# A two-block transformer on one core: split-ahead loads with three blocks of lead, their stores on ScalarE's queue, and another order in the hybrid block

## The chip, the cores and the metric

The kernel runs on one core of one Trainium2 chip, in one launch. The metric is the time of the program on the device in microseconds (us). It was timed three times: 1630.78, 1632.08 and 1635.72 us, with a median of 1632.08. One more execution was taken with the hardware profiler on; the trace and its page are of that one.

## The reference

The input is one sequence of 256 tokens with 1024 features, all float32. Two ordinary layers come first, then one hybrid layer:

```python
for layer in range(2):
    mix = diff_attention(h, ...) if layer == 0 else moba_attention(h, ...)
    h = layer_norm(alpha * h + mix, ln1_g[layer], ln1_b[layer])
    h = layer_norm(alpha * h + relu(h @ w_up[layer]) ** 2 @ w_down[layer],
                   ln2_g[layer], ln2_b[layer])
# hybrid layer
proj = rmsnorm(x, norm1_gain) @ w_in               # 1024 -> 1720 columns
...                                                # NSA and MLA attention on slices of proj
h = x + concat(rmsnorm(o_a), rmsnorm(o_b)) @ w_out
return h + peer_ffn(rmsnorm(h), w_q, sub_keys, u, v)    # top-16 of 16384 experts
```

Here `w_up` is 1024 x 4096 and `w_down` 4096 x 1024 in each layer. The first 416 columns of `w_in` (in the kernel's own order) are the inputs of MLA's low-rank projections `w_uq` and `w_ukv`, then come 24 gates, 512 columns of compressed keys and values, and 768 of NSA queries and keys.

## The kernel before, in words

**Weights.** Every weight block is 128 rows of up to 1024 float32 columns, 512 KB. To keep float32 accuracy on TensorE (PE), a block is split in two: `whi` is a cast on ScalarE (ACT, L415), `wlo = raw - whi` a subtraction on VectorE (DVE, L417), and each product is three matmuls (hi x hi, lo x hi, hi x lo). All blocks stand in one list, `self.plan`. `load_raw` (L449) keeps four raw blocks loaded or on their way, on SyncE's queue (SP). `pump` (L402) splits the next block whenever one of six `whi`/`wlo` buffer pairs is free. Each engine and each queue runs its instructions in the order in which they are written. A `tick` (L324) stands after each block of PE work; it moves background generators one step on.

**The MLP** (`mlp`, L809) runs once in each of the two layers. The up stage is four groups of eight blocks (`proj_F`, L475 to L495 hold the matmuls of the helpers). After each group ACT and DVE evacuate four banks one after the other (relu, square, split into hi and lo). The down stage has 32 blocks (`proj_T`).

**Split ahead.** While the MLP runs, `split_ahead` (L427) prepares blocks that the hybrid block will need in a hurry: nine in each layer, 18 in all. It loads a raw block on SP (L436), waits two ticks, casts it on ACT (L439) and subtracts on DVE (L441), waits a tick, and stores both parts to DRAM on SP (L445), then waits two ticks. That is five ticks a block; nine blocks take the 45 ticks that the MLP gives it. There is one raw buffer and one `hi` buffer. The raw buffer also takes the low part, so the next load has to wait for the store of it.

**The hybrid block** (`hybrid`, L1234) is a planner. Its work is written as generators whose steps name an engine, a modelled cost, the events that they wait for and PSUM banks. `Flow.run` picks the step that can start first by the model, ties by a rank, and emits it; so the ranks and costs set the order of instructions on each engine, and nothing else does. Ahead of the flow stands LayerNorm of the first half of the tokens and a part of the second half's (`norm_add(1, 0)`). In it, `second_norm` does the rest of the second half, `x_split` makes hi and lo of the normalized, transposed input, `dense` runs the projections (first 440 columns, half of the next 512, `w_uq`, `w_ukv`, the other half, the last 768, called A, B and C in `accA` to `accC`), and `weights` emits loads and splits of the blocks, where those prepared ahead come back from DRAM as `whi` and `wlo` (L1218). `residual` makes the scaled input on GpSimd (POOL) and from it `r1`, the RMS factor that `lora` waits for, whose result `w_uq` and `w_ukv` multiply. Where the model sees a gap on PE, `fill` emits dummy matmuls into a spare bank (L1289).

Of the kernel before, what the change touches and what calls it, by code (L numbers as in the profile page):

```python
# [9 lines left out]
F32 = mybir.dt.float32  # L10
# [10 lines left out]
P = 128  # L21
# [256 lines left out]
class Net:  # L278
# [147 lines left out]

    def split_ahead(self, pool, blocks):  # L427

        nc = self.nc
        for b in blocks:  # L430
            src, _ = self.plan[b]
            n = width(src)
            raw = pool.tile([P, 1024], F32, tag="ahead_l", name="ahead")
            hi = pool.tile([P, 1024], F32R, tag="ahead_h", name="ahead")
            to = raw[:, :n]
            nc.sync.dma_start(out=to if len(src.shape) == 2 else to.rearrange("p (c n) -> p c n", c=2), in_=src)  # L436
            yield
            yield
            nc.scalar.copy(out=hi[:, :n], in_=raw[:, :n])  # L439
            lo = raw.bitcast(F32R)  # L440
            nc.vector.tensor_tensor(out=lo[:, :n], in0=raw[:, :n], in1=hi[:, :n], op=ALU.subtract)  # L441
            yield
            self.pre[b] = [self.dram.tile([P, n], F32, name=f"pre{i}_{b}") for i in range(2)]
            for to, of in zip(self.pre[b], (hi.bitcast(F32), raw)):
                nc.sync.dma_start(out=to, in_=of[:, :n])  # L445
            yield
            yield
# [361 lines left out]
    def mlp(self, layer):  # L809
        nc = self.nc  # L810
        self.mark(f"up{layer}")
        with self.tc.tile_pool(name="mlp", bufs=1) as mp:
            hid = Split(mp, "hid", 32, 8)
            b = self.first_hybrid
            self.ahead = self.split_ahead(mp, [b + 2 + layer, *range(b + 11 + 8 * layer, b + 19 + 8 * layer)])
            calls = []

            def pause():
                calls.append(None)
                self.ahead_on = len(calls) < 4  # L820
# [366 lines left out]
    def weights(self, f, end, more, ready, done, extra, cw_ev):  # L1187
# [8 lines left out]
        for b in range(self.split, end + more):  # L1196
# [10 lines left out]
            if parts:  # L1207
                ev = yield "SP", 0.1, (place,), 0
                t = max(t, ev.t) + n * 0.0032
            else:  # L1210
                t = max(t, split[b - 4].t + 2.0 if b - 4 in split else 0.0) + n * 0.0016
                yield on_act(n, (Ev(t if b >= early else 0.0), place))
            self.free[pool] -= 1
# [20 lines left out]
    def hybrid(self, down):  # L1234
# [12 lines left out]
        with ExitStack() as ctx:  # L1247
# [31 lines left out]
            for sl in (slice(0, 256), slice(256, 1024)):  # L1279
                norm_scale(0, sl)  # L1280
            norm_add(1, 0)

            f = Flow(1)
            spare = self.bank()

# [49 lines left out]
            def second_norm():  # L1335
                ev = yield on_dve(512, (Z,))
                sl = slice(512, 1024)
                stt(out=xn[1][:, sl], in0=old[1][:, sl], scalar=ALPHA, in1=down[1][1], op0=mult, op1=add)
                down[0] = down[1] = None
                f.give(2, ev)  # L1340
                yield on_dve(512)
                nc.vector.bn_stats(out=stats[1][0][:, 1, :], in_=xn[1][:, sl])
                yield "DVE", 1.6, None, 0
                norm_rsqrt(1)
                ev = yield on_dve(256, fast=True)
                norm_scale(1, slice(0, 256))
# [39 lines left out]
            def residual():  # L1386
                evs = []
                for th in range(2):
                    after = () if th == 0 else (scaled[1],)
                    for c in range(0, D, 256):  # L1390
# [67 lines left out]
            def dense():  # L1458
# [25 lines left out]

                yield from second(range(4))
                for th in range(2):
                    for i in range(2):
                        ev = yield on_pe(1.04, (ready[b], ready[b + 1], lo_ev[0], lo_ev[1]), 1)
                        acc = self.bank()
                        for k in range(2):  # L1490
# [3 lines left out]
                                     k == 0, k == 1)  # L1494
                        f.add(uq_evac(th, i, acc, ev), 24.5)
                        del acc, w
# [3 lines left out]
                for th in range(2):  # L1500
# [3 lines left out]
                    for i in range(2):  # L1504
                        sl = slice(i * 512, (i + 1) * 512)
                        self.mm3(acc[i], lo.hi(2)[:, halves[th]], lo.lo(2)[:, halves[th]], w[0][:, sl], w[1][:, sl], True, True)
                    f.add(ukv_evac(th, acc, ev), 0)
                    del acc, w
                release(b, ev)
                b += 1  # L1510
                yield from second(range(4, KD))
                for k in range(KD):
# [17 lines left out]
            def lora():  # L1530
# [19 lines left out]
                gates_ev.t = ev.t  # L1550
                f.add(lora_rms(lss, evs), 31)
                banks = None
# [60 lines left out]
            def mla_norms():  # L1613
# [7 lines left out]
                for h in range(2):  # L1621
                    hl = slice(4 * h, 4 * h + 4)
                    kl = slice(8 + 4 * h, 12 + 4 * h)
                    for th in range(2):
# [3 lines left out]
                        self.scale_heads(kr[th].unsqueeze(1).to_broadcast([P, 4, 32]), r[:, th, kl], mqk[th][:, kl, 64:96])  # L1628
                        f.add(mla_heads(8 + 4 * h, th, ev), 5.5)
                        ev = yield on_dve(384, (ev, rope_ev[1][th]))  # L1630
                        self.scale_heads(mqk[th][:, hl], r[:, th, hl])
                        f.add(mla_heads(4 * h, th, ev), 6)

# [88 lines left out]
            def mla_values():  # L1722
                for c in range(4):
# [7 lines left out]
                    if c % 2 == 1:  # L1731
                        f.add(mla_out(c, ob, ev), 27)
                        del ob
# [24 lines left out]
            def values():  # L1758
# [12 lines left out]
                for kv in range(2):  # L1771
                    f.add(windows(kv, ev, blk_ev[kv]), 3.5)
                f.add(compress(blk_ev), 11.5)

            def windows(kv, ev, out):

                yield on_pe(0.44, (ev,), 1)
                ps = self.bank()
# [324 lines left out]
            f.add(gating(), 9)  # L2103
            for th in range(2):
                f.add(k_rope(th), 41.5)
                f.add(q_rope(th), 16)
            f.add(mla_norms(), 2)
            for i in range(8):
                c = i // 4 * 4
                ops = lambda i=i: (mT[:, i, 0:P], mT[:, i, P:S], mT[:, 8 + i, :])  # L2110
                after = [head_ev[d, th] for d in (c, 8 + c) for th in range(2)] + [exp_ev]
                f.add(head(ops, after, (m_ev, m_used, mts), i), 1.5)
            f.add(mla_values(), 14)
            f.add(values(), 2.5)
            for th in range(2):
                f.add(nsa_evac(th), 16)
            f.add(nsa_norms(), 6.5)
            f.add(compressed(), 0.5)
            for i in range(0, 16, 2):
# [3 lines left out]
                gate = [[gates[th][:, 4 * g + j, 1 + br:2 + br] for th in range(2)] for g in range(2)]  # L2123
                f.add(head_pair(ops, (qk_ev[2], qk_ev[j // 2], gate_ev), (n_ev, n_used, nts), i, gate, nsa_rank), 6.5)
            for j in range(4):
                f.add(nsa_values(j), 3)
            f.add(out_dense("b", range(4, 8), end - 8, b_last), 44.5)
            f.add(out_dense("a", range(4), end - 4, a_last), 6.5)
            f.add(mla_update(), 3)
            f.add(last_rms(), 0)  # L2130
            self.xs = None
# [310 lines left out]
    def make_plan(self):  # L2442
# [67 lines left out]
```

## Time and profile before

| what | before |
|---|---|
| median of 3 runs | 1632.08 us |
| the profiled execution | 1632.38 us |
| its span | 1630.6 us |
| PE busy | 1588.0 us, 97% of the span |
| DVE busy, ACT busy, POOL busy | 1122.0, 823.5, 149.4 us |
| granted PE clock, mean | 0.987 of 2.4 GHz |
| DMA, mean over the span | 208 GB/s |

PE's busy time is the sum of its matmul spans; matmuls overlap one another, so the interval between starts tells more than the length of one. The stretches that the change touches are the MLP of layer 0 (about 131 to 316 us), that of layer 1 (438 to 631 us) and the hybrid block (626 to 785 us). After it comes `peer`, with 845 us. A bracket behind a row is idle time of that engine just before the row, and what released it.

### The profile page before, as it was taken

The page shows a single profiled execution, that of the slowest core. Times are in us where ns is not written, and L with a number is a line of the kernel's source. Part 1 is how long each engine was busy: PE and PEld are TensorE (multiplying, and loading weights), DVE is VectorE, ACT ScalarE, POOL GpSimd, SP SyncE. Part 2 cuts the span into 40 slices and gives each one's busy share as a digit, 9 for nine tenths or more (in the row PEclk, how much of TensorE's full clock was granted, in tenths as well). Part 3 has the DMA queues.
Part 4 walks back from the last instruction along what each step waited for, and adds up shares of the span by engine and source line. Part 5 has one row for each costly group of instructions (what it writes and reads, how often), then busy time and mean ns, then how long its engine had stood idle before and what let it go on. Part 6 is the DMA issues. An engine that isn't in the chain of part 4 may idle for free.

```text
span 1630.6 us, 26782 instructions
## 1 busy us (share of the span) xinstructions
PE 1588.0 (97%) x10423; PEld 1428.9 (88%) x10423; DVE 1122.0 (69%) x2108; ACT 823.5 (51%) x1302; POOL 149.4 (9%) x114
## 2 busy tenths in 40 slices
PE   8999999999998999999999999999999999999999
PEld 8879998897898887877999999999999888888887
DVE  5678675677775747876546998767766666666666
ACT  5664564357454645655454444544454544444443
POOL 2000000001000003000027870000000000000000
PEclk9999999999999999999999999999999999999999
DMA  8535768573476776842556766664555677777774
GB/s 297 203 108 169 262 228 285 197 250 94 137 258 220 254 283 215 322 169 69 174 150 196 231 221 208 219 200 151 155 154 182 228 238 245 245 240 237 245 245 154
DMA packets 100319, 339.89 MB, mean 208 GB/s; under 512 B 11120, under 2 KB 16576, under 8 KB 100192
## 3 DMA queue, kind: packets, MB, share of 16 engines
q1 hardware_dynamic: 96400, 326.57, 60.6%
q0 software_dynamic: 3216, 9.51, 2.1%
q10 hardware_dynamic: 576, 2.10, 0.4%
q8 instruction: 81, 1.33, 0.3%
q14 instruction: 46, 0.38, 0.1%
HBM read 303.80 MB, written 34.34 MB: 207 GB/s over the span
## 4 chain that ended last, share of the span: by engine, by line
PE 69%; DVE 15%; DMA 8%; ACT 5%; issue 3%; SPq 1%; ACTq 0%; DVEq 0%
PE ps L475 11%; PE ps L477 11%; PE ps L476 11%; PE ps L490 9%; PE ps L494 9%; PE ps L495 9%; PE ps L2347 4%; DVE wlo L417 3%; DMA ahead<-w_out 2%; DMA pre<-ahead 2%; ACT whi L415 1%; DVE t L2258 1%; DVE t L2253 1%; DVE t L2256 1%; DMA ahead<-w_in 1%
## 5 line engine op out<-in xcount | busy, mean ns | idle before, releaser
L415 ACT CAST whi<-raw 128x1024 fp32r<-128x1024 f32 (+1 forms) x454 | 471.9, 1049 | 482.3 <-PE ps L495 206.4
L417 DVE TENSOR_TENSOR wlo<-raw,whi 128x1024 fp32r<-128x1024 f32 x410 | 497.2, 1223 | 271.4 <-ACT whi L415 270.8
L494 PE MATMUL ps<-x,wlo 128*128 128x256 f32 x1920 | 478.5, 285 | 4.9 <-DVE wlo L417 4.7
L495 PE MATMUL ps<-x,whi 128*128 128x256 f32 x1920 | 477.4, 284 | 0.0
L494 PEld LDWEIGHTS ps<-x,wlo 128*128 128x128 f32 x1920 | 370.8, 193 | 6.1 <-DVE wlo L417 6.1
L495 PEld LDWEIGHTS ps<-x,whi 128*128 128x128 f32 x1920 | 370.7, 193 | 0.0
L490 PE MATMUL ps<-x,whi 128*128 128x256 f32 x1920 | 293.3, 288 | 18.1 <-ACT whi L415 12.5
L475 PE MATMUL ps<-whi,x 128*128 128x512 f32 (+1 forms) x738 | 292.6, 396 | 0.2 <-ACT x L554 0.2
L476 PE MATMUL ps<-wlo,x 128*128 128x512 f32 (+1 forms) x738 | 287.5, 390 | 0.3 <-DVE wlo L420 0.3
L477 PE MATMUL ps<-whi,x 128*128 128x512 f32 (+1 forms) x738 | 287.5, 390 | 0.0
L490 PEld LDWEIGHTS ps<-x,whi 128*128 128x128 f32 x1920 | 256.9, 194 | 20.5 <-ACT whi L415 14.8
L475 PEld LDWEIGHTS ps<-whi,x 128*128 128x128 f32 x738 | 139.8, 189 | 33.9 <-issue 6.2
L477 PEld LDWEIGHTS ps<-whi,x 128*128 128x128 f32 x738 | 139.8, 189 | 30.1 <-DVE x L555 1.1
L476 PEld LDWEIGHTS ps<-wlo,x 128*128 128x128 f32 x738 | 139.8, 189 | 27.7 <-DVE wlo L420 0.6
L417 POOL TENSOR_TENSOR wlo<-raw,whi 128x1024 fp32r<-128x1024 f32 x44 | 106.6, 2423 | 70.8 <-ACT whi L415 70.7
L476 PE MATMUL ps<-wlo,hid 128*128 128x512 f32 x256 | 100.7, 393 | 0.0
L477 PE MATMUL ps<-whi,hid 128*128 128x512 f32 x256 | 100.6, 393 | 0.0
L475 PE MATMUL ps<-whi,hid 128*128 128x512 f32 x256 | 100.6, 393 | 0.0
L2360 DVE TENSOR_TENSOR oh<-iota,rt 128x1024 f16<-128x1024 f16 x64 | 44.1, 690 | 42.2 <-PE ps L2347 42.2
L2347 PE MATMUL ps<-b,oh 128*128 128x128 f16 x512 | 68.3, 296 | 0.0
L476 PEld LDWEIGHTS ps<-wlo,hid 128*128 128x128 f32 x256 | 48.2, 188 | 11.1 <-DVE wlo L417 0.2
L475 PEld LDWEIGHTS ps<-whi,hid 128*128 128x128 f32 x256 | 48.1, 188 | 10.9
(399 smaller groups left out, 1496.9 us busy)
## 6 DMA issues: line engine op xcount, KB each, us to landing
raw<-peer_uT SPq DMA_DIRECT2D x128, 512.0 KB, 3.7
raw<-peer_v SPq DMA_DIRECT2D x128, 512.0 KB, 4.2
raw<-w_up SPq DMA_DIRECT2D x64, 512.0 KB, 5.3
raw<-w_down SPq DMA_DIRECT2D x64, 512.0 KB, 5.0
spill<-ga SPq DMA_DIRECT2D x30, 512.0 KB, 6.0
ga<-spill SPq DMA_DIRECT2D x30, 512.0 KB, 5.3
raw<-w_in_a SPq DMA_DIRECT2D x23, 512.0 KB, 5.7
raw<-w_kv SPq DMA_DIRECT2D x16, 512.0 KB, 4.9
```

Source lines behind the costliest of these rows:

```text
L415: (self.hi_eng or nc.scalar.copy)(out=hi[:, :n], in_=raw[:, :n])
L417: eng.tensor_tensor(out=lo[:, :n], in0=raw[:, :n], in1=hi[:, :n], op=ALU.subtract)
L475: mm(out=out, lhsT=lh, rhs=rh, start=start, stop=False, skip_group_check=skip)
L476: mm(out=out, lhsT=lh, rhs=rl, start=False, stop=False, skip_group_check=skip)
L477: mm(out=out, lhsT=ll, rhs=rh, start=False, stop=stop, skip_group_check=skip)
L490: mm(out=outs[o], lhsT=hi[:, sl], rhs=xs.hi(k), start=k == 0 and o % 2 == 0, stop=False, skip_group_check=True)
L494: mm(out=outs[o], lhsT=lo[:, sl], rhs=xs.hi(k), start=False, stop=False, skip_group_check=True)
L495: mm(out=outs[o], lhsT=hi[:, sl], rhs=xs.lo(k), start=False, stop=k == K - 1, skip_group_check=True)
L2253: nc.vector.max_index(out=idx[:, 0:8], in_max=vals[:, 0:8], in_values=src)
L2256: nc.vector.max(out=vals[:, 8:16], in_=wk)
L2347: nc.tensor.matmul(out=o, lhsT=oh[:, 0, :, t], rhs=b[:, i, :, t], start=i == 0, stop=i == 1)
L2360: nc.vector.tensor_tensor(out=oh, in0=iota.unsqueeze(1).to_broadcast([P, 2, P, 4]), in1=bc(0), op=ALU.is_equal)
```

## The change

In `split_ahead` the load is three ticks ahead of the cast; the store of the high part is issued on ACT right behind the subtraction's emission, that of the low part on ACT one tick later. A block still takes five ticks. The raw tile gets `1 + layer` buffers, so one in layer 0 and two in layer 1. In `hybrid` both halves of the second half's sum and statistics stand ahead of the flow; the flow has three banks from its start and DVE's clock in the model begins at 2.6. Splits of blocks that are already loaded may start at 6.0 in the model, not at 0. All of B stands before `w_uq` and `w_ukv`, in `dense` and in the plan of blocks. The second half of `residual` waits for the last x part. `windows` also waits for `lr_ev` and `lo_ev[2]`. Some 40 ranks change.

```diff
-    def split_ahead(self, pool, blocks):
+    def split_ahead(self, pool, blocks, bufs):
...
-            raw = pool.tile([P, 1024], F32, tag="ahead_l", name="ahead")
+            raw = pool.tile([P, 1024], F32, tag="ahead_l", name="ahead", bufs=bufs)
             hi = pool.tile([P, 1024], F32R, tag="ahead_h", name="ahead")
...
             yield
             yield
+            yield
             nc.scalar.copy(out=hi[:, :n], in_=raw[:, :n])
             lo = raw.bitcast(F32R)
             nc.vector.tensor_tensor(out=lo[:, :n], in0=raw[:, :n], in1=hi[:, :n], op=ALU.subtract)
+            self.pre[b] = [self.dram.tile([P, n], F32, name=f"pre{i}_{b}") for i in range(2)]
+            nc.scalar.dma_start(out=self.pre[b][0], in_=hi.bitcast(F32)[:, :n])
             yield
-            self.pre[b] = [self.dram.tile([P, n], F32, name=f"pre{i}_{b}") for i in range(2)]
-            for to, of in zip(self.pre[b], (hi.bitcast(F32), raw)):
-                nc.sync.dma_start(out=to, in_=of[:, :n])
-            yield
+            nc.scalar.dma_start(out=self.pre[b][1], in_=raw[:, :n])
             yield
...
-            self.ahead = self.split_ahead(mp, [b + 2 + layer, *range(b + 11 + 8 * layer, b + 19 + 8 * layer)])
+            self.ahead = self.split_ahead(mp, [b + 2 + layer, *range(b + 11 + 8 * layer, b + 19 + 8 * layer)], 1 + layer)
...
-                yield on_act(n, (Ev(t if b >= early else 0.0), place))
+                yield on_act(n, (Ev(t if b >= early else 6.0), place))
...
-            norm_add(1, 0)
-
-            f = Flow(1)
             spare = self.bank()
+            for i in range(2):
+                norm_add(1, i)
+            down[0] = down[1] = None
+
+            f = Flow(3)
+            f.now["DVE"] = 2.6
...
             def second_norm():
-                ev = yield on_dve(512, (Z,))
-                sl = slice(512, 1024)
-                stt(out=xn[1][:, sl], in0=old[1][:, sl], scalar=ALPHA, in1=down[1][1], op0=mult, op1=add)
-                down[0] = down[1] = None
-                f.give(2, ev)
-                yield on_dve(512)
-                nc.vector.bn_stats(out=stats[1][0][:, 1, :], in_=xn[1][:, sl])
-                yield "DVE", 1.6, None, 0
+                yield "DVE", 1.6, (Z,), 0
                 norm_rsqrt(1)
...
-                    after = () if th == 0 else (scaled[1],)
+                    after = () if th == 0 else (scaled[1], xready[1][KD - 1])
...
-                yield from second(range(4))
+                yield from second(range(KD))
...
-                    f.add(ukv_evac(th, acc, ev), 0)
+                    f.add(ukv_evac(th, acc, ev), 2)
...
-                yield from second(range(4, KD))
...
-                yield on_pe(0.44, (ev,), 1)
+                yield on_pe(0.44, (ev, lr_ev, lo_ev[2]), 1)
...
             f.add(second_norm(), 0)
             for th in range(2):
-                f.add(transposed(th), 0.5)
+                f.add(transposed(th), 6)
                 for c in range(KD):
-                    f.add(x_split(th, c), 14.5)
-            f.add(residual(), 0)
-            f.add(dense(), 9.5)
-            f.add(self.weights(f, end, 3, ready, done, extra, cw_ev), 4)
-            f.add(lora(), 4)
+                    f.add(x_split(th, c), 9.5)
+            f.add(residual(), 6)
+            f.add(dense(), 9)
+            f.add(self.weights(f, end, 3, ready, done, extra, cw_ev), 20)
+            f.add(lora(), 8)
...
-        self.add_pairs(A["w_in_2"], 440, 952, range(2))
+        self.add_pairs(A["w_in_2"], 440, 952, range(4))
         add(A["w_uq"], 0, 768, range(2))
         add(A["w_ukv"], 0, 1024, range(1))
-        self.add_pairs(A["w_in_2"], 440, 952, range(2, 4))
```

## Rows read from the trace of the kernel before

**Rows 1.** The page: busy us (share of the span) and instructions of each engine.

```profile
PE 1588.0 (97%) x10423; PEld 1428.9 (88%) x10423; DVE 1122.0 (69%) x2108; ACT 823.5 (51%) x1302; POOL 149.4 (9%) x114
```

**Rows 2.** Who TensorE waited for: us in total, times, longest.

```profile
PE ps L490 <- ACT whi L415: 12.5, 7, 6.0
```

**Rows 3.** PE's timeline, up stages: start, us, engine, line, form, [idle before <-releaser].

```profile
131.55 1.19 PE L490 MATMUL ps<-x,whi 128*128 128x256 f32 x8
...
229.54 0.39 PE L475 MATMUL ps<-whi,hid 128*128 128x512 f32 x1
...
438.66 1.20 PE L490 MATMUL ps<-x,whi 128*128 128x256 f32 x8
...
441.61 1.10 PE L490 MATMUL ps<-x,whi 128*128 128x256 f32 x8
...
455.82 1.11 PE L490 MATMUL ps<-x,whi 128*128 128x256 f32 x8
...
508.10 2.07 PE L490 MATMUL ps<-x,whi 128*128 128x256 f32 x8 [5.97 <-ACT whi L415]
...
542.87 0.39 PE L475 MATMUL ps<-whi,hid 128*128 128x512 f32 x1
```

**Rows 4.** Windows: length, busy of PE, PEld, DVE, ACT, POOL, clock, DMA share, GB/s.

```profile
510.00:515.00 5.00, 5.00 (x36) 5.00 (x36) 3.56 (x4) 1.94 (x2) 0.00 (x0) 0.78 0.80 230
...
515.00:520.00 5.00, 5.00 (x45) 5.00 (x44) 0.39 (x1) 0.00 (x0) 0.00 (x0) 1.00 0.97 384
```

**Rows 5.** ACT's timeline around a group's end in layer 1.

```profile
496.47 1.05 ACT L439 CAST ahead<-ahead 128x1024 fp32r<-128x1024 f32 x1 [7.17 <-DMA ahead<-w_out]
...
498.37 0.59 ACT L830 ACTIVATE relu<-ps 128x512 f32<-128x512 f32 x1
...
507.01 3.88 ACT L415 CAST whi<-raw 128x1024 fp32r<-128x1024 f32 x4
```

**Rows 6.** Waits of ACT and SP, layer 1; of ACT, layer 0.

```profile
ACT ahead L439 <- DMA ahead<-w_out: 33.8, 7, 7.2
...
SPq L436 <- DMA pre<-ahead: 19.3, 6, 4.1
...
ACT ahead L439 <- DMA ahead<-w_in: 20.8, 7, 5.5
```

**Rows 7.** DMA issues: KB each, median us to landing; ACT's own, ns.

```profile
ahead<-w_out SPq DMA_DIRECT2D x8, 512.0 KB, 5.4
...
L2165 ACTq DMA_DIRECT2D hscr<-h x2: 344/395/446, 788.7 to 789.1; - x2
```

**Rows 8.** PE's timeline at the start of the hybrid block.

```profile
631.35 0.40 PE L477 MATMUL ps<-whi,hid 128*128 128x512 f32 x1
...
652.71 0.39 PE L475 MATMUL ps<-whi,x 128*128 128x512 f32 x1
...
659.40 0.34 PE L475 MATMUL ps<-whi,lo 128*128 128x384 f32 x1
...
665.49 1.50 PE L1289 MATMUL ps<-k_c_ident 128*128 128x128 f32 x12
...
668.65 0.40 PE L475 MATMUL ps<-whi,x 128*128 128x512 f32 x1
...
674.11 0.40 PE L475 MATMUL ps<-whi,x 128*128 128x512 f32 x1
```

**Rows 9.** DVE's timeline there.

```profile
634.23 1.50 DVE L1224 TENSOR_TENSOR wlo<-raw,whi 128x1024 fp32r<-128x1024 f32 x1
...
637.05 1.21 DVE L1224 TENSOR_TENSOR wlo<-raw,whi 128x1024 fp32r<-128x1024 f32 x1
...
649.02 0.29 DVE L1380 TENSOR_TENSOR x<-tofy,x 128x128 fp32r<-128x128 f32 x1 [0.25 <-ACT x L1378]
...
653.37 0.16 DVE L390 SCALAR_TENSOR_TENSOR r<-ra_t,ra_y 128x2 f32<-128x2 f32 x1
```

**Rows 10.** POOL's last operation of the residual.

```profile
647.28 0.73 POOL L1395 TENSOR_TENSOR h<-h,lnbc 128x256 f32<-128x256 f32 x1
```

More of the change, by code (lines that the diff above doesn't have):

```diff
@@ L1494, in dense @@
                                      k == 0, k == 1)
-                        f.add(uq_evac(th, i, acc, ev), 24.5)
+                        f.add(uq_evac(th, i, acc, ev), 16.5)
                         del acc, w
@@ L1550, in lora @@
                 gates_ev.t = ev.t
-                f.add(lora_rms(lss, evs), 31)
+                f.add(lora_rms(lss, evs), 34)
                 banks = None
@@ L1628, in mla_norms @@
                         self.scale_heads(kr[th].unsqueeze(1).to_broadcast([P, 4, 32]), r[:, th, kl], mqk[th][:, kl, 64:96])
-                        f.add(mla_heads(8 + 4 * h, th, ev), 5.5)
+                        f.add(mla_heads(8 + 4 * h, th, ev), 3.5)
                         ev = yield on_dve(384, (ev, rope_ev[1][th]))
                         self.scale_heads(mqk[th][:, hl], r[:, th, hl])
-                        f.add(mla_heads(4 * h, th, ev), 6)
+                        f.add(mla_heads(4 * h, th, ev), 2)
             def mla_heads(c, th, ev):
@@ L1731, in mla_values @@
                     if c % 2 == 1:
-                        f.add(mla_out(c, ob, ev), 27)
+                        f.add(mla_out(c, ob, ev), 45)
                         del ob
@@ L1771, in values @@
                 for kv in range(2):
-                    f.add(windows(kv, ev, blk_ev[kv]), 3.5)
-                f.add(compress(blk_ev), 11.5)
+                    f.add(windows(kv, ev, blk_ev[kv]), 25)
+                f.add(compress(blk_ev), 3.5)
             def windows(kv, ev, out):
-                yield on_pe(0.44, (ev,), 1)
+                yield on_pe(0.44, (ev, lr_ev, lo_ev[2]), 1)
                 ps = self.bank()
@@ L2095, in hybrid @@
             for th in range(2):
-                f.add(transposed(th), 0.5)
+                f.add(transposed(th), 6)
                 for c in range(KD):
-                    f.add(x_split(th, c), 14.5)
-            f.add(residual(), 0)
-            f.add(dense(), 9.5)
-            f.add(self.weights(f, end, 3, ready, done, extra, cw_ev), 4)
-            f.add(lora(), 4)
-            f.add(gating(), 9)
+                    f.add(x_split(th, c), 9.5)
[3 more added lines that the diff above has]
+            f.add(lora(), 8)
+            f.add(gating(), 23.5)
             for th in range(2):
-                f.add(k_rope(th), 41.5)
-                f.add(q_rope(th), 16)
-            f.add(mla_norms(), 2)
+                f.add(k_rope(th), 43.5)
+                f.add(q_rope(th), 3.5)
+            f.add(mla_norms(), 8.5)
             for i in range(8):
@@ L2111, in hybrid @@
                 after = [head_ev[d, th] for d in (c, 8 + c) for th in range(2)] + [exp_ev]
-                f.add(head(ops, after, (m_ev, m_used, mts), i), 1.5)
-            f.add(mla_values(), 14)
-            f.add(values(), 2.5)
+                f.add(head(ops, after, (m_ev, m_used, mts), i), 8)
+            f.add(mla_values(), 19.5)
+            f.add(values(), 4)
             for th in range(2):
-                f.add(nsa_evac(th), 16)
-            f.add(nsa_norms(), 6.5)
-            f.add(compressed(), 0.5)
+                f.add(nsa_evac(th), 26)
+            f.add(nsa_norms(), 3.5)
+            f.add(compressed(), 2.5)
             for i in range(0, 16, 2):
@@ L2123, in hybrid @@
                 gate = [[gates[th][:, 4 * g + j, 1 + br:2 + br] for th in range(2)] for g in range(2)]
-                f.add(head_pair(ops, (qk_ev[2], qk_ev[j // 2], gate_ev), (n_ev, n_used, nts), i, gate, nsa_rank), 6.5)
+                f.add(head_pair(ops, (qk_ev[2], qk_ev[j // 2], gate_ev), (n_ev, n_used, nts), i, gate, nsa_rank), 2.5)
             for j in range(4):
[L2126 to L2130, printed above, removed]
+                f.add(nsa_values(j), 1.5)
+            f.add(out_dense("b", range(4, 8), end - 8, b_last), 66.5)
+            f.add(out_dense("a", range(4), end - 4, a_last), 5)
+            f.add(mla_update(), 7.5)
+            f.add(last_rms(), 8)
             self.xs = None
```

## The prediction

> **What bounds the kernel now.** I read in this order: the page's busy shares, who TensorE (PE) waited for, PE's timeline, the clock in windows, and last the ACT, DVE and SP queues at those places. PE is busy 97% of the span [rows 1], so only where it idles or runs at the lower clock is there time to win. Most of its waiting is one line: the split of a weight block on ScalarE (L415) was late for `proj_F`, 12.5 us in 7 waits [rows 2]. That is in the two up stages of the MLP. The rest worth having is at the start of the hybrid block, where PE runs dummy matmuls (L1289) or idles while the second LayerNorm half is made.
>
> The up stages can be priced without guessing what a wait cost. Five undisturbed blocks take 455.82 - 441.61 = 14.21 us, 2.84 a block, so 32 blocks 90.9 us. Layer 1's stage lasts 542.87 - 438.66 = 104.2 us: 13.3 too long. Layer 0's lasts 229.54 - 131.55 = 98.0: 7.1 too long [rows 3]. The largest hole shows what is in it: PE waits 5.97 us before 508.10, and behind it the granted clock is 0.78 in 510 to 515: of its two levels the lower one, 1.2 GHz, until about 512, which costs another 2 us [rows 3, 4].
>
> Why the split was late: ACT reaches the cast of an ahead block (L439) and stands 7.17 us for its load; one weight cast later it begins the four relu evacuations, 498.37 to 507.01, in which no weight block is cast [rows 5]. PE eats three blocks in those 8.6 us. Six whi/wlo pairs exist, one of them in use, so five blocks should lie ready; two blocks of slack (5.7 us) were eaten by the 7.17. The load was late because it waited on SP for the store of the block before to leave the one raw buffer (L436, 19.3 us in 6 waits, [rows 6]), and only two blocks of PE work lay between its issue and its cast. All such ACT waits, the down stages' with them: 33.8 us in 7 behind w_out in layer 1, 20.8 in 7 in layer 0 [rows 6].
>
> **Part 1: loads, lead and buffers in layer 1.** The period stays five ticks a block, so no tick and no byte is added. Load to cast becomes three ticks, 3 x 2.84 = 8.5 us, against a median landing of 5.4 us for these loads [rows 7]; with two raw buffers the load no longer waits for a store. The ACT wait of up to 7.2 us should go to nearly none, which restores the 5.7 us of slack before each evacuation. Late next would be an ordinary raw load. Of the 13.3 us excess I take 11.5 off; bounds 0 (another wait takes the place) and 13.3. The same waits in the down stage lie beside a busy PE, and their going is worth nothing.
>
> **Part 2: layer 0.** There the buffer count stays 1. The low store is emitted at tick 4 and the next load at tick 5, so SP now stands for that store to land: if it lands like the loads, in 5.4 us [rows 7], at least 5.4 - 2.84 = 2.6 us, with the ordinary raw loads queued behind it. The load then has 8.5 less this wait, and a cast meets it about on time where ACT now waits 20.8 / 7 = 3.0 us each [rows 6]. A smaller gain: 4 of the 7.1; bounds -3 (raw loads late, one hole of layer 0's kind more) and 7.1.
>
> **Part 3: stores on ACT's queue.** 36 stores leave SP for ACT. The only ACT-issued DMAs before cost 0.34 to 0.45 us [rows 7]; the high store also waits for its own cast to drain. That makes about 0.8 us of ACT per ahead block, 14.4 us in all, in stages where ACT is half idle. The low store waits for DVE's subtraction, but one tick later, when that operation (1.2 to 1.5 us for one of its shape, [rows 9]) is done. Queued behind it on ACT are weight casts, so if it were held PE would feel it after the slack. Cost 0; bounds 0 and all 14.4 on the path. SP's freedom from stores I price at nothing too.
>
> **Part 4: the hybrid's head.** The added norm (two DVE operations) was already first on DVE in the flow, so emitting it before costs and gains nothing by itself. What changes is the planner's picture: DVE starts at 2.6, and weight casts for loaded blocks may not start before 6.0. Two such splits now stand on DVE in front of the first x parts, 1.50 and 1.21 us [rows 9], and two casts on ACT. Without them all of the x parts come 2.7 us earlier, the last at about 646.3 instead of 649.0. PE follows: the first projection ends at 652.71 now [rows 8]; I expect 649. The second half of the residual on POOL now waits for the last x part, which spares DVE its company. But it then ends later: its eight operations, 0.73 us each [rows 10], make it 652.3 instead of 648.0. r1 came 5.5 us after it (653.53, [rows 9]), which with an emptier ACT I put at 4.5: r1 at 657 instead of 653.5. The uq matmuls followed r1 by 6 us (659.40, [rows 8]). So they start at about 662. Cover for this: the whole second projection stands there now, with 5.5 us of work that lay at 668.65 to 674.11 [rows 8]. From 649 its 11 us reach to 660, so PE is left without work for some 2 us. The 12 dummy matmuls at 665.49 mark a wait for the ukv banks, 1.5 us, and the higher rank of that evacuation should shorten it to nothing. The last projection (C), which starts at 674.11 now, then starts at 662 + 4.1 (uq: 24 matmuls of 384 columns at three quarters of the 0.2275 us that one of 512 takes, 5.46 / 24 [rows 8]) + 3.5 (ukv) = about 670, 4 us earlier.
>
> Gain 4 us. Bounds: at that spacing the 48 matmuls of 440 columns in the first projection need at least 9.4. The down stage's last matmul starts at 631.35 [rows 8]; with the transposes the projection could end at 642, so no more than some 10 us can be won there. Upwards: the new ranks reorder some 30 more steps, nearly all behind C, whose matmuls stay the same and whose cover I cannot follow step by step. Their likeliest effect I take as 0. The worst I allow is one hole more of the kind before 508.10, 8 us with its half clock [rows 3, 4], so 8 - 4 = +4 for the stage, and +8 without the head's gain.
>
> **Sum.** The profiled execution took 1632.38 us (span 1630.6 and 1.8 around it), 0.3 above the median of 1632.08. 1632.4 - 11.5 - 4 + 0 - 4 = 1612.9, so 1613. Behind the hybrid PE never starves on anything that the change touches, so the earlier start is kept to the end.
>
> **Rivals.**
>
> (a) The MLP's holes go, but the hybrid's new order gives back its gain and 4 more: 1632.4 - 15.5 + 4 = 1621. For it: the late r1 and the many ranks. Against: two splits really leave the front.
>
> (b) Layer 0 stays as it is or worsens, since its one raw buffer now has a shorter time from store to load, and layer 1 gains half: 1632.4 - 6.7 - 4 = 1622. For it: SP's in-order wait. Against: ACT needs to be over 5 us late before PE notices.
>
> (c) The transfers are the bound in the up stages: an earlier request waits in the queue as long as the later one did, so only the hybrid's 4 us remain: 1628. For it: 0.97 of the DMA time is used in 515 to 520 [rows 4]. Against: that slice is followed by emptier ones, and ACT's waits begin with SP's.
>
> The Trainium skill's page "DMA: Bandwidth & Descriptors", section "Issuing engines are not separate DMA queues", speaks for (c) against the part of the change that moves stores: a second issuing engine saves only its issue time, as all transfers share the same 16 engines. By it the move is worth nothing by itself, and the gain must come from lead and buffer.
>
> (d) Slower: the low store, issued in order on ACT at the first tick of a group, holds the casts behind it. It decides once a store holds ACT over 3 us (issue, DVE's subtraction, the queue). Then each of the six inner group boundaries repeats the hole of 508.10, 5.97 and some 2 us at half clock: 48 us in place of today's 20.4, so +27.6, less the hybrid's 4: 1656. For it: ACT is in order and has the evacuations there. Against: 0.45 us an issue [rows 7].
>
> (e) The lead changes nothing and the order of the hybrid nothing: 1632. It would need ACT's waits on ahead loads to stay.
>
> **How the numbers follow.** Forecast 1604 to 1618: 0.60. (a) 0.13, (b) 0.10, (c) 0.05, (d) 0.03, (e) 0.03; the last 0.06 is below 1604, where nearly all of the 20.4 us goes and the head gains over 5. For 8 in 10 I take 1603 to 1622, which holds the forecast with (a) and (b). About 0.3%, 4.9 us, is what a measurement of this kernel tells from none, so faster is below 1627.2: 0.60 + 0.13 + 0.10 + 0.06 and a part of (c) give 0.91; within 0.05; slower 0.04.
>
> **What would show it.** ACT's waits on L439 in the up stages near zero; no PE wait over 1 us on L415 there and no clock dip; up stages of about 92.7 (layer 1) and 94 us (layer 0); ACT-queue DMAs of 0.3 to 0.5 us. In the hybrid: no L1222 cast before the first x casts, the first projection some 17.5 us long from the end of the down stage instead of 21.1, and C's start 4 us earlier relative to it. Wrong: an SP wait in layer 0 that starves raw loads, ACT standing on L445's successor, or a longer stretch from C's end to the flow's end.

## The result, and the profile after

The changed kernel takes 1613.93 us (median of 4 runs, 1612.06 to 1616.18), the kernel before, on the same chip, 1631.43 (4 runs): ratio 0.9889, 95% interval 0.9866 to 0.9911. The forecast was 1613. The profiled execution took 1613.41 us, its span 1611.6, at a mean clock of 0.997.

The page's busy row, and who waited in the whole span (us in total, times, longest), answer [rows 1, 2, 6]:

```profile
PE 1578.6 (98%) x10433; PEld 1418.9 (88%) x10433; DVE 1124.0 (70%) x2108; ACT 825.5 (51%) x1302; POOL 147.9 (9%) x114
```

```profile
ACT ahead L440 <- DMA ahead<-w_in: 11.3, 5, 3.5
...
PE ps L490 <- ACT whi L415: 5.8, 5, 2.2
...
ACT ahead L440 <- DMA ahead<-w_out: 4.5, 3, 1.7
```

ACT's waits behind w_out went from 33.8 us to 4.5, and PE's wait for late splits from 12.5 to 5.8. PE's timeline of the two up stages, first and last row of each and the largest holes, answers [rows 3]:

```profile
131.36 1.20 PE L490 MATMUL ps<-x,whi 128*128 128x256 f32 x8
...
193.32 0.86 PE L490 MATMUL ps<-x,whi 128*128 128x256 f32 x5 [1.91 <-ACT whi L415]
...
225.98 0.39 PE L475 MATMUL ps<-whi,hid 128*128 128x512 f32 x1
...
435.30 1.20 PE L490 MATMUL ps<-x,whi 128*128 128x256 f32 x8
...
497.50 1.21 PE L490 MATMUL ps<-x,whi 128*128 128x256 f32 x8 [2.15 <-ACT whi L415]
...
530.30 0.39 PE L475 MATMUL ps<-whi,hid 128*128 128x512 f32 x1
```

The up stages last 225.98 - 131.36 = 94.6 us and 530.30 - 435.30 = 95.0, where they lasted 98.0 and 104.2. The hole of 5.97 us is now one of 2.15, and the clock does not fall behind it, as the windows beside [rows 4] show (length; busy of PE, PEld, DVE, ACT, POOL; clock, DMA share, GB/s):

```profile
495.00:500.00 5.00, 2.80 (x21) 2.39 (x21) 4.06 (x6) 4.14 (x6) 0.00 (x0) 1.00 0.34 114
500.00:505.00 5.00, 5.00 (x44) 5.00 (x44) 2.99 (x3) 1.34 (x2) 0.00 (x0) 1.00 0.81 265
```

The 19.0 us between the two spans are: layer 0's up stage -3.4, layer 1's -9.2, the hybrid block from the last down matmul to the start of peer -6.5 (153.1 to 146.6 us), the rest +0.1. One profile of a stage is uncertain: four kernels with the MLP of the change gave 93.5 to 94.6 us in layer 0 and 94.9 to 97.4 in layer 1, two with that of before 98.0 and 99.1, and 104.2 and 101.4.

### The profile page after: what moved, and what is told of

Its sections match the earlier page's. It is cut to its first block, busy times and chain, and to the rows that moved or that the text cites. A ratio compares the mean times of both kernels' runs of the same rounds, so it can differ in the third digit from the quotient of the medians.

```text
span 1611.6 us, 26809 instructions
## 1 busy us (share of the span) xinstructions
PE 1578.6 (98%) x10433; PEld 1418.9 (88%) x10433; DVE 1124.0 (70%) x2108; ACT 825.5 (51%) x1302; POOL 147.9 (9%) x114
## 4 chain that ended last, share of the span: by engine, by line
PE 72%; DVE 15%; ACT 5%; DMA 5%; issue 2%; SPq 0%; ACTq 0%; DVEq 0%
PE ps L475 13%; PE ps L477 13%; PE ps L476 13%; PE ps L494 9%; PE ps L490 9%; PE ps L495 9%; PE ps L2342 4%; DVE wlo L417 3%; ACT whi L415 2%; DMA ahead<-w_in 1%; DVE t L2253 1%; DMA ahead<-w_out 1%; DVE t L2248 1%; DVE t L2251 1%; DVE t L2250 1%
## 5 line engine op out<-in xcount | busy, mean ns | idle before, releaser
L490 PE MATMUL ps<-x,whi 128*128 128x256 f32 x1920 | 290.7, 287 | 11.3 <-ACT whi L415 5.8
L475 PEld LDWEIGHTS ps<-whi,x 128*128 128x128 f32 x738 | 139.0, 188 | 33.8 <-issue 5.3
```

The lines of the kernel that those rows point to most:

```text
L475: mm(out=out, lhsT=lh, rhs=rh, start=start, stop=False, skip_group_check=skip)
L490: mm(out=outs[o], lhsT=hi[:, sl], rhs=xs.hi(k), start=k == 0 and o % 2 == 0, stop=False, skip_group_check=True)
```

## The experiments

**One half of the change at a time.** m_all has the new `split_ahead` and its buffer count with the hybrid block of before; h_all is the changed kernel with the old `split_ahead`.

> The MLP part of the change alone (three ticks of lead, two raw buffers in layer 1, stores on ACT), hybrid block as before. If the two parts add up: up stages 94.6 us (layer 0) and 95.0 (layer 1) as after, hybrid block 153.1 as before, profiled time about 1620. If part of the hybrid's gain came from the MLP's new state (earlier loads, other queue), its 153.1 would fall to 150 or less here.

> The hybrid part alone, MLP as before. If the parts add up: up stages 98.0 and 104.2 us as before, hybrid block 146.6 as after, profiled time about 1626. If the hybrid's gain rests on the MLP's part, the block stays over 150.

m_all took 1618.52 us, ratio 0.9925 (0.9904 to 0.9946); h_all 1624.81, ratio 0.9965 (0.9953 to 0.9977). Against 1630.46 that is -11.9 and -5.7 us, together -17.6, and the whole change gives -17.5. Both halves are real, and they add up. The hybrid block took 151.0 us in m_all and 148.2 in h_all, so neither of the 153.1 and 146.6 that the expectations name. The kernels from here to h_r1 were timed once each, in the execution that was profiled.

**What in the MLP half does it.** Four kernels carry parts of it. m_lead and m_leadbufs keep the stores on SP:

```diff
             ...
+            yield                # m_lead, m_leadbufs: load to cast three ticks
             nc.scalar.copy(out=hi[:, :n], in_=raw[:, :n])
             ...
-            yield
```

and m_leadbufs has two raw buffers in layer 1 besides. m_act moves the stores alone, with two ticks of lead and one buffer; m_onebuf is m_all without the second buffer:

```diff
-            for to, of in zip(self.pre[b], (hi.bitcast(F32), raw)):
-                nc.sync.dma_start(out=to, in_=of[:, :n])
+            nc.scalar.dma_start(out=self.pre[b][0], in_=hi.bitcast(F32)[:, :n])     # m_act, m_onebuf
+            yield
+            nc.scalar.dma_start(out=self.pre[b][1], in_=raw[:, :n])
```

> Before, with three ticks of lead alone; one raw buffer and stores on SP in both layers. Theory (ACT stands on the ahead load): layer 1's up stage falls from 104.2 to 97 to 100 us, as the lead is longer but the single buffer still holds the load on SP; layer 0's to 95. Rival (SP's stores and the load's wait for them hold back the ordinary raw loads): stores still on SP, so 103 or more in layer 1 and 97 or more in layer 0.

> Before, with lead and two raw buffers in layer 1, stores left on SP. Theory: the queue of the stores is worth nothing, up stages within 1 us of those after the change, 94.6 and 95.0. Rival (stores on SP hold back the raw loads): layer 1 at 98 or more, layer 0 at 97 or more.

> The kernel before with the 36 stores on ScalarE's queue and nothing else: the load still has two ticks of lead and one raw buffer. The factor that is still missing beside lead alone (up stages 97.1 and 103.8 us) and lead with buffers (98.1 and 101.3). Theory 1, the stores' place is nearly all of it, and it needs neither lead nor buffer: up stages of 93.5 to 95.5 (layer 0) and 95 to 97 (layer 1), span 1615.5 to 1619. Theory 2, the prediction's, lead and buffers are the cure and the place only lets them work: layer 1 stays at 100 or more, because the load still waits for the store to leave the one buffer and is cast two ticks later.

> The MLP part with three ticks of lead and the stores on ScalarE's queue, but one raw buffer in layer 1 too (the kernel before's order of the hybrid block). With the second buffer layer 1's up stage took 94.9 us, with ScalarE's waits for ahead loads 6.4 us; layer 0, with one buffer, 93.5 and 6.0. Theory 1, lead and the stores' place do it together and the second buffer is spare: layer 1 at 94 to 97 us, waits 6 to 9. Theory 2, blocks of 512 KB need the second buffer: layer 1 at 98 to 101, waits 10 to 14.

Three more ask what is wrong with stores on SP. m_hold is m_all with a store of 8 columns on SP where the stores stood; m_mid and m_late are m_leadbufs (two high halves too in layer 1) with each pair of stores emitted directly ahead of the next ahead load, or one tick behind it. Below, with lines left out at the dots, `store()` is the pair of stores of the block before:

```diff
+            nc.sync.dma_start(out=self.dram.tile([P, 8], F32, ...), in_=raw[:, :8])     # m_hold
```

```python
            if bufs == 2:                              # m_mid
                store()
            nc.sync.dma_start(out=to ..., in_=src)
            yield
            ...
            nc.sync.dma_start(out=to ..., in_=src)     # m_late
            yield
            if bufs == 2:
                store()
            ...
```

> The MLP part of the change whole, stores on ScalarE's queue (up stages 93.5 and 94.9), with one added store of 4 KB (8 columns of the low half) on SP at the place where the stores stood before: SP waits for the same cast and subtraction as before, but hardly any byte goes through its queue. Theory hold: the up stages go back to 96.5 to 99 (layer 0) and 99 to 103 (layer 1). Theory ring: they stay at 93 to 95.5 and 94 to 96.5.

> Lead and two buffers (of the high half too in layer 1), all stores left on SP, but in layer 1 each pair of stores is emitted one tick after the NEXT ahead load, some three ticks after its own cast: SP then has nothing to wait for at them, while the same 1 MB a block still goes through the same queue. Layer 0 is as in lead with buffers (98). Theory hold, SP stands in order at stores whose cast is not done and issues the loads behind them late: layer 1's up stage falls from 101.3 to 94.5 to 97, as with the stores on ScalarE's queue. Theory ring, loads queue behind the stores' bytes in the same queue: layer 1 stays at 100 to 103, and the median landing of the ahead loads stays near 8 us.

> As the kernel with late stores (lead, two buffers and two high halves in layer 1, all stores on SP; its layer 1 up stage 95.1 us, ScalarE's waits for ahead loads 9.1 us there), but with each pair of stores emitted directly ahead of the next ahead load and no longer one tick behind it: two ticks after its own cast, so SP has little to wait for, but 1 MB of stores stands ahead of the load in the same queue. Theory order (the bytes of the stores ahead of the load in its queue are the larger part): layer 1's up stage 99 to 102 us, ScalarE's waits for ahead loads 12 us or more, median landing about 8 us. Theory hold (only SP's standing counts, the order in the queue does not): 94.5 to 97, waits 7 to 10 us.

The table takes the up stages from PE's timeline, ACT's waits for ahead loads from the waits of those stretches, and the median landing of layer 1's 512 KB ahead loads from the DMA issues there. The last two columns are the issue and the cast of the third ahead block, counted from the start of layer 1's up stage (before: 490.50 and 496.47 less 438.66). It is the block in front of the largest hole.

| kernel | up 0 | waits | up 1 | waits | landing | issue | cast |
|---|---|---|---|---|---|---|---|
| before | 98.0 | 14.0 | 104.2 | 20.8 | 6.8 | 51.8 | 57.8 |
| h_all (MLP of before) | 99.1 | 16.3 | 101.4 | 17.8 | 5.5 | 51.8 | 56.2 |
| m_lead | 97.1 | 11.7 | 103.8 | 16.2 | 3.8 | 51.3 | 55.4 |
| m_leadbufs | 98.1 | 10.6 | 101.3 | 14.0 | 8.4 | 45.9 | 54.2 |
| m_mid | 97.5 | 11.3 | 100.0 | 15.4 | 8.5 | 45.8 | 54.0 |
| m_act | 97.9 | 12.8 | 100.2 | 13.9 | 6.5 | 49.6 | 54.2 |
| m_late | 98.7 | 11.6 | 95.1 | 9.1 | 6.8 | 45.9 | 51.7 |
| m_hold | 96.0 | 7.8 | 96.3 | 7.7 | 7.1 | 45.4 | 51.8 |
| m_onebuf | 93.1 | 3.9 | 96.4 | 8.1 | 6.2 | 48.9 | 52.4 |
| m_all | 93.5 | 6.0 | 94.9 | 6.4 | 7.3 | 43.3 | 51.0 |
| after | 94.6 | 6.8 | 95.0 | 6.5 | 6.5 | 45.1 | 51.7 |

m_lead and m_leadbufs came out as the rivals said and not as the prediction's theory (103.8 and 97.1; 101.3 and 98.1); m_onebuf as theory 1 (96.4 us, 8.1 of waits). The times go with the stages (the kernel before beside them: 1629.62 to 1631.25 us): 1629.10 us for m_lead, 1627.60 for m_leadbufs and 1626.07 for m_mid, but 1621.05 for m_late, 1621.04 for m_hold and 1621.34 for m_onebuf.

Three things follow.

*No single part does it; lead and the move of the stores together do* (in layer 1 also lead, two buffers and stores on SP behind the load, m_late). In layer 0 lead alone (four kernels, 97.1 to 98.7) and the move alone (97.9) give nothing against 98.0 and 99.1; both give 93.1 to 94.6. In layer 1 lead alone (103.8), lead with two buffers (101.3) and the move alone (100.2) stay within or close to the 101.4 to 104.2 of the old MLP; lead and move give 96.4 (m_onebuf), and with the second buffer it is 94.9 to 97.4, so that buffer is worth nothing that shows. m_act meets theory 2 in its number (100.2, "100 or more") and only half in its reason: in layer 1's up stage SP's wait for the store to leave the one buffer fell from 10.2 us in 3 to 2.6 in 1, but the ahead loads landed after 6.5 us (median) with two ticks, 5.7 us, to do it in, and ACT still waited 13.9. (Its one time, 1634.29 against 1629.62, has more in it: its down stages were 3.1 us longer than before, and everything behind the MLP 2.8. I did not settle why.)

*In layer 0, lead alone is taken from the store.* The period stays five ticks, so a tick more between load and cast is a tick less between store and next load, and with one buffer SP stands that much longer at the load. Its wait there was 10.3 us in 3 in layer 0 of the kernel before; in m_leadbufs this is SP's row (us, times, longest):

```profile
SPq L436 <- DMA pre<-ahead: 22.0, 4, 7.2
```

m_all gives up the same tick and waits 14.2 us in 3. What the move adds shows at the third block. On SP its stores stand behind five raw loads, which wait for raw buffers, and the next ahead load waits for the stores to land; on ACT the low store goes out some 5 us earlier in the stage, and the load 6.0 us earlier (65.2 against 71.2). SP in m_leadbufs, then ACT and SP in m_all:

```profile
180.73 15.40 SPq L457 DMA_DIRECT2D raw<-w_up  x5
196.18 0.90 SPq L446 DMA_DIRECT2D pre<-ahead  x2
...
202.81 0.33 SPq L436 DMA_DIRECT2D ahead<-w_in  x1
```

```profile
191.60 0.33 ACTq L446 DMA_DIRECT2D pre<-ahead  x1
```

```profile
197.02 0.42 SPq L436 DMA_DIRECT2D ahead<-w_in  x1
```

At the stores themselves SP's waits list nothing in the up stages of any kernel that has them on SP.

*In layer 1, two buffers turn a wait of SP into a wait in the queue.* The wait on L436 is gone there in m_leadbufs, and the third load is issued 5.9 us earlier in the stage (51.8 to 45.9), but it is cast only 2.0 to 3.6 earlier. m_mid and m_late differ in one thing, whether the stores of the block before stand ahead of the load in SP's queue or behind it. SP's queue of m_mid, then of m_late:

```profile
483.57 0.90 SPq L437 DMA_DIRECT2D pre<-ahead  x2
484.51 0.91 SPq L447 DMA_DIRECT2D ahead<-w_out  x1
```

```profile
485.56 0.42 SPq L445 DMA_DIRECT2D ahead<-w_out  x1
486.39 0.33 SPq L470 DMA_DIRECT2D raw<-w_up  x1
486.77 0.98 SPq L437 DMA_DIRECT2D pre<-ahead  x2
```

ACT's cast of that block in m_mid, then in m_late, with the idle time before it:

```profile
492.72 1.05 ACT L451 CAST ahead<-ahead 128x1024 fp32r<-128x1024 f32 x1 [6.09 <-DMA ahead<-w_out]
```

```profile
491.29 1.05 ACT L451 CAST ahead<-ahead 128x1024 fp32r<-128x1024 f32 x1 [3.72 <-DMA ahead<-w_out]
```

From issue to cast it is 8.2 us behind the stores and 5.7 ahead of them. The difference, 2.5 us, is about what 1 MB would take at the 384 GB/s of [rows 4] (2.7, an estimate). PE pays for it in the hole that follows, 4.38 against 2.11 us, and the stage ends at 100.0 against 95.1: the theory of order was right for m_mid, and the theory of the hold for m_late was right in its number only. The hold by itself (m_hold) shows in layer 0: with hardly a byte of stores on SP, SP's wait at the next load is 21.4 us in 5, as in m_leadbufs, and the stage takes 96.0 us with 7.8 of waits, against 93.1 to 94.6 and 3.9 to 6.8. That lies between the ranges of both theories (96.5 to 99, and 93 to 95.5); with the bytes on SP too it is 98.1 (m_leadbufs). In layer 1, with two buffers, SP's wait at that load is 0.3 us in m_hold and there is nothing to hold; 96.3 is inside the spread.

**The hybrid's head.** h_early lets the splits of loaded blocks start at 0.0 again in the planner's picture, h_r1 takes away the residual's new wait:

```diff
-                yield on_act(n, (Ev(t if b >= early else 6.0), place))
+                yield on_act(n, (Ev(t if b >= early else 0.0), place))     # h_early
-                    after = () if th == 0 else (scaled[1], xready[1][KD - 1])
+                    after = () if th == 0 else (scaled[1],)                # h_r1
```

> The changed kernel with the splits of loaded blocks allowed from 0.0 instead of 6.0 in the planner's picture, nothing else. The prediction's account of the hybrid's head (two splits leave the front of the x parts, 2.7 us): the first projection's last matmul goes back from 18.8 us after the down stage to 20.5 to 21.5, and the last projection (C) starts 1.5 to 3 us later than 40.5. Rival, the splits cost nothing there because the norm emitted ahead is what moved the x parts: the first projection ends at 18.3 to 19.3 and C starts within 1 us of 40.5; the whole within 1.5 us of the changed kernel.

> The changed kernel without the second half of the residual's wait for the last x part, nothing else. It began its uq matmuls 32.3 us after the down stage's last matmul (before 28.0 in its profile, 27.5 in kernels with the old order), C 40.5 after. The prediction's account (that wait makes r1 late and with it uq; DVE is spared POOL's company in return): r1 and uq 1.5 to 4 us earlier, uq at 28.5 to 31, C 0 to 2 us earlier, the x parts 0 to 1 us later. Rival, uq is late because the second projection was put whole ahead of it: uq stays at 31.5 to 33 and C within 0.7 us.

The table gives the start of A's last matmul, of the first uq matmul, of C's first matmul of 256 columns (0.7 us behind its first) and of peer; h_all and v_lead4 have the changed kernel's hybrid block as it is.

| from the last down matmul, us | A's end | uq | C | peer |
|---|---|---|---|---|
| before | 21.2 | 28.0 | 43.5 | 153.1 |
| eight other kernels with the old order | 18.7 to 19.6 | 27.5 to 29.0 | 42.9 to 43.5 | 148.9 to 153.1 |
| after | 18.8 | 32.3 | 40.5 | 146.6 |
| h_all | 19.8 | 33.3 | 41.5 | 148.2 |
| v_lead4 (below) | 18.6 | 32.1 | 40.3 | 147.0 |
| h_early | 19.6 | 33.3 | 41.1 | 146.9 |
| h_r1 | 21.7 | 33.8 | 42.6 | 147.3 |

h_early is 0.8 us behind the changed kernel at A's end and 0.6 at C, nearer to the rival, but h_all, without those splits in front and at a clock of 1.00, stands at the same 19.8 and 41.5: a cost of the splits is not shown. Nor does the clock settle it: in these 41 us it was 0.92 in h_early, but in v_lead4 0.96, with the earliest A and C of the table. h_r1 went against both theories: without the wait r1 alone came earlier (19.9 us after the last down matmul, against 22.9), and A, uq and C came later.

**A version with more lead.** v_lead4 is the changed kernel with four ticks of lead in layer 1.

```diff
+            if bufs == 2:
+                yield
             nc.scalar.copy(out=hi[:, :n], in_=raw[:, :n])
             ...
             nc.scalar.dma_start(out=self.pre[b][1], in_=raw[:, :n])
-            yield
+            if bufs == 1:
+                yield
```

> The changed kernel with four ticks of lead in place of three in layer 1 (two raw buffers there; the period stays five ticks; layer 0, with one buffer, keeps three). Theory 1, what is left of layer 1's excess (95.0 us against 90.9 for 32 undisturbed blocks) still comes from ScalarE's waits for ahead loads, 6.5 us of them: another tick, 2.84 us a block, takes 3 to 5 us of the waits, layer 1's up stage falls to 92 to 94, the whole is 1 to 3 us below the changed kernel (1611 to 1613.5), layer 0 stays at 93 to 95. Theory 2, the waits are under the slack now and what is left has other reasons: waits fall but the stage stays at 94.5 to 97.

It took 1611.31 us (4 runs), ratio 0.9872 (0.9852 to 0.9892), which can't be told from the changed kernel's 0.9889. ACT's waits for ahead loads in layer 1 fell from 6.5 us to 0.2, yet the stage took 95.2: theory 2. Part of that fall is the place of a cast: the tick moves the third block's cast on ACT from in front of the evacuations (487.00, the first relu at 488.45 in the changed kernel) to behind them, where its load has long landed:

```profile
485.14 0.59 ACT L833 ACTIVATE relu<-ps 128x512 f32<-128x512 f32 x1
...
495.49 1.05 ACT L442 CAST ahead<-ahead 128x1024 fp32r<-128x1024 f32 x1
```

What is late now is an ordinary raw load. ACT's waits in 430 to 527 us, and PE's one hole left there:

```profile
ACT whi L415 <- DMA raw<-w_up: 17.7, 12, 3.2
```

```profile
520.48 0.74 PE L493 MATMUL ps<-x,whi 128*128 128x256 f32 x4 [2.04 <-ACT whi L415]
```

The same wait was 11.9 us in 7 in the changed kernel. What ACT no longer waits for ahead loads, it waits for raw loads in the same queue.

## Why the prediction was right, and where its steps were wrong

**What bounds the kernel** held: the hole behind a group's end came from ACT standing at an ahead load. In all 22 stages of the table PE's excess over 90.9 goes with ACT's wait: up to 9.1 us of waits, 93.1 to 96.4; from 10.6 to 17.8, 97.1 to 103.8; 20.8, 104.2. Under that the relation ends: v_lead4 has 0.2 us of waits and takes 95.2. Of the signs that the prediction names, the waits did not go to near zero (6.8 and 6.5 us), a hole of over 1 us is left in each up stage (1.91 and 2.15), and layer 1 stands at 95.0 and not at 92.7.

**Parts 1 and 2** had the sizes nearly (forecast -11.5 and -4, measured -9.2 and -3.4) and the cause wrong: by them lead and buffer alone should have brought layer 1 to about 92.7, and they brought it to 101.3. In layer 0 SP's wait for the store was 12.3 us in 3, 4.1 each, where the prediction had at least 2.6, and ACT still waited 6.8 us for loads that it had about on time. "With two raw buffers the load no longer waits for a store" is true of SP's issue only. "Late next would be an ordinary raw load" came true once the ahead loads were on time, in v_lead4.

**Part 3 is the step that failed.** "Cost 0" was right as a cost: the stores take 0.33 us of ACT each, with 0.4 to 0.5 us more where the next operation stands behind a high store. "SP's freedom from stores I price at nothing too" was wrong. With lead and buffers in place the move is worth 101.3 - 94.9 = 6.4 us in layer 1 and 98.1 - 93.5 = 4.6 in layer 0 (m_leadbufs, m_all), 3.9 and 3.5 against the slowest profiles of the same MLP (97.4 and 94.6), and 1627.6 - 1618.5 = 9.1 us in the times: most of the 11.9 that the MLP half gains. The sentence drawn from the Trainium skill ("DMA: Bandwidth & Descriptors", section "Issuing engines are not separate DMA queues"), that by it "the move is worth nothing by itself", holds for m_act in layer 0, 97.9 against 98.0; beside lead and buffers the measurement decides against it. That the engines are shared did not make the place of a store free here: on SP a store goes out behind raw loads that wait for buffers, which makes the load into a single buffer late (layer 0), and a load directly behind 1 MB of stores in the queue landed later (layer 1). Rival (c) had the second of these; rival (d) did not come: no hole of its kind stands at a group's end. At the third block the changed kernel casts at 487.00, issues the high store at 488.08 and the low one only at 495.97, behind the four evacuations.

**Part 4** came out at -6.5 us in the profiles, forecast -4, by steps that were mostly wrong. PE's rows answer [rows 8] (the last down matmul, A's first, B's first, dummies, uq, C):

```profile
619.40 0.40 PE L477 MATMUL ps<-whi,hid 128*128 128x512 f32 x1
...
622.88 0.45 PE L475 MATMUL ps<-whi,x 128*128 128x440 f32 x1
...
638.38 0.40 PE L475 MATMUL ps<-whi,x 128*128 128x512 f32 x1
...
650.20 1.73 PE L1292 MATMUL ps<-k_c_ident 128*128 128x128 f32 x14
651.69 0.42 PE L475 MATMUL ps<-whi,lo 128*128 128x384 f32 x1
...
659.87 0.28 PE L475 MATMUL ps<-whi,x 128*128 128x256 f32 x1
```

DVE's answer [rows 9]:

```profile
631.30 1.43 DVE L1224 TENSOR_TENSOR wlo<-raw,whi 128x1024 fp32r<-128x1024 f32 x1
...
635.40 1.21 DVE L1224 TENSOR_TENSOR wlo<-raw,whi 128x1024 fp32r<-128x1024 f32 x1
636.53 0.69 DVE L1376 TENSOR_TENSOR x<-tofy,x 128x128 fp32r<-128x128 f32 x3
...
642.29 0.16 DVE L390 SCALAR_TENSOR_TENSOR r<-ra_t,ra_y 128x2 f32<-128x2 f32 x1
```

- *The splits leave the front of the x parts*: they left the front, but two still stand ahead of the last x part. It is done at 637.22, 17.8 us after the last down matmul; before 18.0. A's end moved by 2.4 us in the two profiles, of which most belongs to the one profile of the kernel before, with its stretch at the lower of the two clock levels (0.50 in 640 to 645): in the eight other kernels with the old order A ends at 18.7 to 19.6, and with the new order as it is at 18.6 to 19.8. No gain at A's end is shown.
- *POOL waits for the last x part, r1 comes 3.5 us late*: POOL does not wait. Its last residual operation ends at 635.00, before the last x part; that of [rows 10] ended 16.7 us after the last down matmul, this one 15.6. The new event is one of the planner's picture only. What it orders is ACT: the two square sums over 1024 columns now stand behind the x casts, r1 is ready 22.9 us after the last down matmul (before 22.0), and in h_r1 the sums come first and the last x casts and x parts wait for them. ACT in h_r1, then in the changed kernel:

```profile
637.03 1.04 ACT L1149 ACTIVATE rjunk<-h 128x1024 f32<-128x1024 f32 x1
...
638.20 1.06 ACT L1149 ACTIVATE rjunk<-h 128x1024 f32<-128x1024 f32 x1
...
639.25 0.28 ACT L1374 CAST x<-tofy 128x128 fp32r<-128x128 f32 x1
```

```profile
635.93 0.69 ACT L1374 CAST x<-tofy 128x128 fp32r<-128x128 f32 x3
636.52 2.00 ACT L1222 CAST whi<-raw 128x1024 fp32r<-128x1024 f32 x2
638.41 1.06 ACT L1149 ACTIVATE rjunk<-h 128x1024 f32<-128x1024 f32 x1
```

  I had priced as a loss what, in one profile of h_r1, is worth 1.9 to 3.1 us at A's end and 1.1 to 2.3 at C, against the three kernels that keep the wait; at peer's start nothing of it shows (147.3 against 146.6 to 148.2).
- *uq 2.6 us later in the block, PE without work for some 2 us before it, C 4 us earlier*: 4.2 later, 1.5 us of dummies, C 3.0 earlier. By these rows the whole second projection ahead of uq is what moves it: B runs for 11 us behind A, and in h_r1, with r1 ready 3 us earlier, uq starts no earlier.
- *The ranks behind C are worth 0*: from C to peer it is 106.1 us where it was 109.6. The kernel before idles and falls to the lower clock there; the first two windows are of it, the third of the changed kernel:

```profile
710.00:715.00 5.00, 2.58 (x16) 1.70 (x13) 4.39 (x14) 2.57 (x6) 0.00 (x0) 0.85 0.46 184
...
725.00:730.00 5.00, 4.43 (x22) 3.14 (x21) 3.31 (x30) 0.96 (x2) 0.00 (x0) 0.72 0.75 299
```

```profile
713.00:718.00 5.00, 5.00 (x40) 3.99 (x39) 4.25 (x18) 3.11 (x10) 0.00 (x0) 1.00 0.48 174
```

  m_late, with the old order, had the same idle time at a full clock there (5.7 us of PE in both), and took 106.0 us from C to peer. By this one profile the order itself is worth nothing behind C, as forecast, and what came on top, which the forecast did not have, is the clock: the new order about halves that idle time (2.9 us in the changed kernel), and the falls are gone (0.97 or 0.98 from C to the flow's last transposes in eight of nine kernels with the old order, 1.00 in all five with the new one).

So it is partly luck that the sum came within 1 us: an overestimate of the MLP half (-15.5, measured -11.9 by its times) met an underestimate of the hybrid half (-4, measured -5.7), and the base, the profiled 1632.4, lay 1.0 us above the median of 1631.43.

What stays open: why m_act was slow outside the up stages, how the move's worth in layer 0 divides between the late load and the bytes, and how much of the hybrid's gain is order and how much the clock that follows it.

## What to carry to other kernels

Count a prefetch's lead from what its issue waits for, not from the place in the program: in a fixed period a tick of lead is taken from somewhere, here from the store in front of the next load. When a wait is cured by a buffer, look at what then stands ahead of the transfer in its queue; here stores that are not urgent did best on another queue, or behind the load. An event given to a planner is a rank and not a wait: read from the trace which engine's order it changes before pricing it.

## What was not expected of the hardware

A load of 512 KB issued directly behind 1 MB of stores on the same queue landed after 8.5 us (median), and 6.8 when the stores came behind it; with the stores on ACT and the same lead it was 6.2 to 7.6. The median alone is no proof of it, as v_lead4, with four ticks of lead and no store in that queue, shows 8.3. A store of 4 KB (m_hold) landed after 5.4 us, no sooner than stores of 384 KB in the kernel before (5.3). With three ticks of lead and the stores on ACT's queue, the third ahead block of layer 1 was cast 51.0 to 52.4 us into the stage whether its load was issued at 43.3 or at 48.9: an earlier issue bought next to nothing there.
